# Sixteen experts of a mixture-of-experts stage: the overflow block cut into four short branches, the weight splits taken out of them

## The chip, the cores and the metric

The kernel runs on one core of one Trainium2 chip. The metric is the device time of one launch in microseconds (us), the median of three runs. A profiled execution of the same program gives the trace from which the rows below are taken; its times are read from the start of the profile's span.

## The reference

One layer: differential attention, then a mixture of experts in two levels, both with pre-RMSNorm, modulation and a residual, then a last RMSNorm. The part that the change touches is the mixture of experts over 1024 tokens of 1024 values:

```python
g_idx = jnp.argmax(g_logits, axis=-1)                 # one of 4 groups
top_v, top_i = lax.top_k(e_sel, EXPERT_TOP_K)         # 2 of the 4 experts in that group
hid = jax.nn.silu(jnp.einsum('td,edf->tef', t, w_gate)) * jnp.einsum('td,edf->tef', t, w_up)
hid = hid * gates.astype(hid.dtype)[:, :, None]
y = jnp.einsum('tef,efd->td', hid, w_down)            # 16 experts, d = 1024, f = 512
...
x = x + g2[:, None, :] * y
return rmsnorm(x, norm_final)
```

All inputs are float32. Each token goes to two experts, so 2048 pairs of token and expert are worked on.

## The kernel before

Attention and routing come first (765 us of the span) and are not touched. Then the sixteen experts run one after the other. For expert e the kernel knows the number n of its tokens only at run time, as a register on every engine.

**Slots.** An expert has 128 slots in a main block and 64 more in a small block (M2 = 64); a third block, a loop of 128 slots at a time (over_loop), is there for n > 192. GpSimd gathers the rows of the tokens from h2d by an indirect DMA into xgxa (main) and xgxb (small). A slot without a token points to one of 128 spare rows at the end of h2d and accd, so empty slots are gathered and scattered like full ones. The result of a block, times g2, is added into accd by an indirect DMA with accumulation (scatter_add).

**Pieces.** The weights of an expert come as 12 pieces of 128x1024 float32 (512 KB each): 0 to 3 are gate and up for the first half of f, 4 to 7 for the second half, 8 to 11 are down. Each piece lands in a raw buffer (wraw, 12 of them, NRAW) and is split into a high part whi (a cast on ScalarE, split_hi) and a low part wlo (raw minus high, split_lo), so that TensorE can multiply in three passes of its faster float32r form. The low parts are made by VectorE, but for pieces 8 and 11, which GpSimd makes (PLO). A load into a raw buffer is issued on SyncE's queue once the split that read the buffer is done (split_done, raw_to). The split parts live in 14 slots taken from two pools (slot_tiles).

**One expert on TensorE** (block): 48 matmuls gu of the first half, 48 of the second, with the transposes of the next expert's tokens (xpose) and the matmuls for the slot indices (slots_mm) in between; then the transposes tp of the gated hidden values (hid), and 12 matmuls py of down for each half. What the other engines do meanwhile is placed by hooks: a list of (count, function), where the count is the number of gu matmuls that have been written, so the program's order on every engine is written out by hand. SPL is the table of hooks for the pieces of the next expert, EVAC, SMM, OH, XPH, GAT and CNT are counts of other hooks.

**The branch** (L1531). After the second gu, one conditional (tc.If, n > 128) holds the whole rest of the expert in two arms. The arm that is taken runs the small block woven into the rest of the main block, with two piece splits, the final multiply by g2 on GpSimd and the nested conditional of over_loop (L1475); the Else arm runs the rest of the main block and the same two splits. After both arms two more pieces are split, and the other eight of the next expert are done in its SPL hooks. A hint (mark_branch_hint_location) tells TensorE's sequencer ahead of time where the conditional will go.

**The last expert** (e = 15) runs beside the final RMSNorm: after the last scatter into accd, eight blocks of accd are loaded (norm_load), squared and summed on ScalarE (norm_sum), scaled on VectorE and stored.

## Time and profile before

| what | value |
| --- | --- |
| median of 3 runs | 1263.29 us (1252.71 to 1267.82) |
| the profiled execution, its own time | 1262.4 us |
| the profiled execution, its span | 1260.6 us |
| TensorE busy over the span | 1123.9 us (89%) |
| VectorE busy | 936.9 us (74%) |
| ScalarE busy | 732.4 us (58%) |
| GpSimd busy | 387.0 us (31%) |
| DMA over the span | 205.22 MB, 163 GB/s |

A busy share is an average over the whole span. The experts start at 765.26 us, when the first gu matmul starts, and the last of them starts at 1210.38 us; those two times are the starts of gu matmuls in the timeline of TensorE. The page's chain of waits holds only the last microsecond (a scatter on GpSimd), so the stage has to be read from windows, from the table of waits and from timelines. In a windows row the columns are the length, then for each engine busy us and instructions, then the granted TensorE clock (1.00 is the full level), the mean busy share of the 16 DMA engines, and GB/s. Engines: PE is TensorE, PEld its weight loads, DVE VectorE, ACT ScalarE, POOL GpSimd, SP SyncE; a q behind a name is that engine's sequencer.

### The profile page before, as it was taken

Reading aid. Unit: us, or ns where it says so; the run is one execution under the profiler, and the core shown is the slowest. Engines: PE = TensorE matmul, PEld = TensorE weight load, DVE = VectorE, ACT = ScalarE, POOL = GpSimd, SP = SyncE. Lnnn points to the kernel's source line nnn. Section 1 sums busy time; section 2 is a strip of 40 time slices with the busy share of each in tenths; the row PEclk is TensorE's granted clock in tenths of the full one; section 3 lists DMA queues with packets and bytes.
Section 4 is the critical chain, followed back from the end, with each engine's and each line's share of the span. In section 5 each row is a group of like instructions: output and inputs, shape, how many; then the busy total and the mean of one; then the engine's idle time right before and its main releaser. Section 6 shows DMA issues by size and latency. Waiting matters only on the chain. (4 is left out here: it accounts for less than half of the span.)

```text
span 1260.6 us, 18887 instructions
## 1 busy us (share of the span) xinstructions
PE 1123.9 (89%) x6816; PEld 938.1 (74%) x6816; DVE 936.9 (74%) x1494; ACT 732.4 (58%) x1218; POOL 387.0 (31%) x335
## 2 busy tenths in 40 slices
PE   6989999999999999998999976888888888888982
PEld 6767777777777777776778866787787877788771
DVE  4768788888988677778765567688686867667754
ACT  5465767676676666678553323566464656535544
POOL 3011020111111010116024115545465764435532
PEclk8899999999999999999999987999999988999996
DMA  9612023322323000114238536799697999679737
GB/s 328 197 45 85 22 85 92 94 90 82 92 77 109 30 26 26 42 35 137 76 127 284 187 120 224 239 300 322 209 316 216 335 297 322 194 214 267 203 92 278
DMA packets 153278, 205.22 MB, mean 163 GB/s; under 512 B 11652, under 2 KB 122917, under 8 KB 153138
## 3 DMA queue, kind: packets, MB, share of 16 engines
q1 hardware_dynamic: 146432, 179.86, 44.6%
q0 software_dynamic: 6512, 23.06, 7.8%
q8 instruction: 75, 1.23, 0.4%
q14 instruction: 65, 0.53, 0.1%
q10 hardware_dynamic: 194, 0.54, 0.1%
HBM read 175.77 MB, written 27.67 MB: 161 GB/s over the span
## 5 line engine op out<-in xcount | busy, mean ns | idle before, releaser
L1132 DVE TENSOR_TENSOR wlo<-wraw,whi 128x1024 fp32r<-128x1024 f32 x155 | 218.2, 1456 | 33.3 <-issue 17.7
L1386 PE MATMUL gu<-whi,XT 128*128 128x256 f32 x1216 | 211.8, 287 | 3.9 <-DVEq L1475 3.9
L1127 ACT CAST whi<-wraw 128x1024 fp32r<-128x1024 f32 x192 | 188.3, 1048 | 28.3 <-PE py L1418 23.2
L499 ACT ACTIVATE E<-E,mn 128x1024 f32<-128x1024 f32 x128 | 147.1, 1151 | 84.0 <-DVE mn L496 83.8
L1386 PEld LDWEIGHTS gu<-whi,XT 128*128 128x128 f32 x1216 | 176.7, 195 | 8.0 <-ACTq L1475 6.4
L496 DVE CUSTOM_DVE_ANT_0 E<-S,negd 128x1024 f32<-128x1024 f32 x128 | 152.8, 1220 | 19.4 <-PE S L491 18.8
L1386 PE MATMUL gu<-wlo,XT 128*128 128x256 f32 x704 | 152.2, 294 | 14.0 <-DVE wlo L1132 12.5
L143 POOL TENSOR_TENSOR wl<-wraw,wh 128x1024 fp32r<-128x1024 f32 x21 | 50.4, 2399 | 333.6 <-ACT wh L142 293.2
L297 PE MATMUL mm<-hH,wh 128*128 128x512 f32 x336 | 139.2, 414 | 2.1 <-DVE V L397 2.1
L297 PE MATMUL mm<-hL,wh 128*128 128x512 f32 x336 | 140.3, 417 | 0.0
L297 PE MATMUL mm<-hH,wl 128*128 128x512 f32 x336 | 138.6, 412 | 0.0
L1132 POOL TENSOR_TENSOR wlo<-wraw,whi 128x1024 fp32r<-128x1024 f32 x37 | 98.4, 2662 | 91.2 <-ACT whi L1127 91.1
L1386 PEld LDWEIGHTS gu<-wlo,XT 128*128 128x128 f32 x704 | 111.9, 195 | 18.3 <-DVE wlo L1132 16.4
L526 ACT CAST aH<-tp 128x512 fp32r<-128x512 f32 x128 | 74.0, 578 | 73.8 <-PE tp L524 73.5
L510 DVE SCALAR_TENSOR_TENSOR E<-E,r 128x1024 f32<-128x1024 f32 x64 | 85.8, 1341 | 27.8 <-ACT E L508 26.2
L1418 PE MATMUL py<-whi,hid 128*128 128x512 f32 x256 | 95.2, 432 | 10.1 <-issue 6.3
L527 DVE TENSOR_TENSOR aL<-tp,aH 128x512 fp32r<-128x512 f32 x128 | 88.0, 687 | 17.2 <-ACT aH L526 16.0
L524 PE MATMUL tp<-ident,E 128*128 128x128 f32 x512 | 78.3, 276 | 10.5 <-DVE aL L527 7.2
L524 PEld LDWEIGHTS tp<-ident,E 128*128 128x128 f32 x512 | 62.3, 141 | 33.6 <-DVE aL L527 13.7
L706 PE MATMUL mm<-wo,wh 128*128 128x512 f32 x240 | 79.6, 406 | 1.3 <-ACT mm L718 1.3
L297 PEld LDWEIGHTS mm<-hH,wh 128*128 128x128 f32 x336 | 63.4, 189 | 18.3 <-issue 5.1
L297 PEld LDWEIGHTS mm<-hL,wh 128*128 128x128 f32 x336 | 63.4, 189 | 17.2 <-issue 8.3
(348 smaller groups left out, 2355.4 us busy)
## 6 DMA issues: line engine op xcount, KB each, us to landing
wraw<-in_expert_w_gate SPq DMA_DIRECT2D x64, 512.0 KB
wraw<-in_expert_w_up SPq DMA_DIRECT2D x64, 512.0 KB
wraw<-in_expert_w_down SPq DMA_DIRECT2D x64, 512.0 KB
aw<-in_ada_w SPq DMA_DIRECT2D x64, 256.0 KB
wraw<-in_attn_w_in SPq DMA_DIRECT2D x23, 512.0 KB
ld<-in_ada_w SPq DMA_DIRECT2D x32, 256.0 KB
ld<-in_x SPq DMA_DIRECT2D x8, 512.0 KB
xt<-in_x SPq DMA_DIRECT2D x8, 512.0 KB
```

The lines of the kernel that those rows point to most:

```text
L297: nc.tensor.matmul(pq, w[:, k], t[k][:, n], start=(k == 0 and i == 0), stop=(k == KT - 1 and i == 2))
L496: nc.vector.tensor_tensor_reduce(out=e, in0=sps[m], in1=negd[:, w0:w0 + S], op0=OP.add, op1=OP.min, scale=-slope, scalar=3.0e38, accum_out=mn)
L499: nc.scalar.activation(e, e, AF.Exp, bias=mn, scale=-1.0, accum_out=sm)
L510: nc.vector.scalar_tensor_tensor(es[0], es[1], r2, es[0], op0=OP.mult, op1=OP.add)
L524: nc.tensor.transpose(pt[:, i], a[:, k * P:(k + 1) * P], ident)
L526: nc.scalar.copy(th[:, kk * 4:kk * 4 + 4, q], pt)
L527: nc.vector.tensor_tensor(tl[:, kk * 4:kk * 4 + 4, q], pt, f(th[:, kk * 4:kk * 4 + 4, q]), op=OP.subtract)
L706: nc.tensor.matmul(py, w[:, h], wt[h][:, ns], start=(h == 0 and s == 0), stop=(h == H - 1 and s == 2))
L1127: nc.scalar.copy(WP[e, i][0], RAW[e, i])
L1132: eng.tensor_tensor(low, RAW[e, i], f(high), op=OP.subtract)
L1386: nc.tensor.matmul(pg[:, i], XT[:, xi, k], w[:, k % 4], start=(k == 0 and xi == 0 and wi == 0 and i == 0), stop=(k == KT - 1 and (xi, wi) ...
L1418: nc.tensor.matmul(py[n], hT[:, xi, i], WP[e, 8 + hf * 2 + i][wi][:, n * 512:(n + 1) * 512], start=(hf == 0 and j == 0), stop=(hf == 1 and ...
```

## The change

- The single conditional is replaced, for experts 0 to 14, by five: over_loop's own (L1486, not taken unless n > 192), now ahead of the small block, and four short ones (all on L1548, function small) that hold only instructions of the small block: (a) its transposes, (b) its first gu, (c) its second gu, the first half of its down and the hid of both, (d) the second half of its down, the multiply by g2 and the scatter. (d) is written into the next expert, at count DSM = 12. The rest of the main block and all splits stand outside. The hint goes to over_loop's conditional; the four short ones have none.
- Six pieces of the next expert are split around the short branches (two ahead of b, two behind b, two behind c); the other six in hooks at counts 0 to 90.
- The 14 slots are made once and used as a ring; there are 11 raw buffers in place of 12.
- All low parts are made by VectorE, so are both halves of the main block's multiply by g2 (before: one half by ScalarE and GpSimd), and the small block's.
- Gathers and scatters get bounds_check = 1023, so the spare rows of empty slots are not moved. The extra 1024 slots of the 3072 that 2048 pairs leave empty are the ones concerned.

The core of the diff:

```diff
-    NRAW = 12
+    NRAW = 11
-    SMM = 80
-    OH = 40
-    NARM = 2
+    SMM = 92
+    OH = 66
...
+    RING = []
     def slot_tiles():
-        pool, nb = (mwr, NEARLY) if nslot[0] % NSLOT < NEARLY else (mw, NSLOT - NEARLY)
-        nslot[0] += 1
-        return [pool.tile([P, 1024], F32R, name=n, bufs=nb) for n in ("whi", "wlo")]
+        j = nheld[0] % NSLOT
+        if j == len(RING):
+            pool = mwr if j < NEARLY else mw
+            RING.append([pool.tile([P, 1024], F32R, name="%s%d" % (n, j)) for n in ("whi", "wlo")])
+        return RING[j]
...
-        eng = eng or (nc.gpsimd if i in PLO else nc.vector)
+        eng = eng or nc.vector
...
-    EVAC = 52
-    N0 = 20
-    SPL = [(0, split_hi, 4), (0, split_lo, 4), (0, split_hi, 5), (0, split_lo, 5), (2, split_hi, 6), (3, split_hi, 7),
-           (30, split_lo, 6), (48, split_hi, 8), (48, split_lo, 8), (50, split_lo, 7), (50, split_hi, 10), (50, split_lo, 10),
-           (69, split_hi, 9), (70, split_lo, 9), (72, split_hi, 11), (80, split_lo, 11)]
+    EVAC = 60
+    DSM = 12
+    N0 = 28
+    SPL = [(0, 6), (24, 7), (56, 8), (64, 9), (80, 10), (90, 11)]
...
+            nc.gpsimd.indirect_dma_start(out=xg[:m], out_offset=None, in_=h2d,
+                                         in_offset=bass.IndirectOffsetOnAxis(ap=idx[:m, b:b + 1], axis=0),
+                                         bounds_check=S - 1, oob_is_err=False)
...
+        over_loop(e, XT, n)
+        s1 = gate(pg1, tt[:, 0, 3:4], P)
+        pt = small_pt()
+        small(lambda: small_evac(small_pe(xs, pt), XT))
+        d = down(e, py, 0, h0, P)
+        take(d, 9)
+        h1 = hid(s1, P)
+        run(d)
+        splits(2)
+        sl, hs = mp.tile([P, 256], F32, name="sl"), mp.tile([P, 2, 2, P], F32R, name="hs")
+        pg = gu_tile()
+        small(lambda: gate(run(gu(e, XT, 0, M2, pg=pg)), g, M2, xs[:, 0:512], sl))
+        splits(2)
+        run(down(e, py, 1, h1, P))
...
+        def small_c():
+            hid(sl, M2, hT=hs)
+            gate(run(gu(e, XT, 1, M2, pg=pg2)), g, M2, xs[:, 512:1024], sl)
+            run(down(e, spy, 0, hs, M2))
+            hid(sl, M2, hT=hs)
+
+        def small_d():
+            for n in range(2):
+                run(down(e, spy, 1, hs, M2, (n,)))
+                fold(spy, oyo, n)
+                r = slice(n * 512, (n + 1) * 512)
+                v.tensor_tensor(oyo[:M2, r], oyo[:M2, r], g2b[:M2, r], op=OP.mult)
+            scatter_add(idx[:M2, 1:2], oyo[:M2])
+
+        small(small_c)
+        splits(2)
+        later.append((DSM, lambda: small(small_d)))
...
-            v.tensor_tensor(yo[:, 0:512], py[0], g2b[:, 0:512], op=OP.mult)
...
-                nc.gpsimd.tensor_tensor(yo[:, 512:1024], yo[:, 512:1024], g2b[:, 512:1024], op=OP.mult)
+            for n in range(2):
+                v.tensor_tensor(yo[:, n * 512:(n + 1) * 512], py[n], g2b[:, n * 512:(n + 1) * 512], op=OP.mult)
```

On VectorE, from the gate of the second half (sl) on, this stood in the Else arm and behind the join of the two arms before; wlo is a split's low part, the L1531 row is the end of the conditional:

```order
L1399 SCALAR_TENSOR_TENSOR sl<-sl,tt,gu 128x256
L1409 TENSOR_TENSOR hid<-tp,hid 128x256
L1132 TENSOR_TENSOR wlo<-wraw,whi 128x1024 x2
L1531 UNCONDITIONAL_BRANCH
L1132 TENSOR_TENSOR wlo<-wraw,whi 128x1024 x5
L1242 TENSOR_SCALAR rk<-rk 128x192 x8
```

and this stands there now, from hid on; the L1548 rows are the short conditionals b and the start of c:

```order
L1419 TENSOR_TENSOR hid<-tp,hid 128x256
L1134 TENSOR_TENSOR wlo_7452<-wraw,whi_7451 128x1024
L1134 TENSOR_TENSOR wlo_7466<-wraw,whi_7465 128x1024
L1548 COMPARE_AND_BRANCH
L1406 TENSOR_TENSOR xgxb<-xgxb,gu 64x512
L1409 SCALAR_TENSOR_TENSOR sl<-sl,tt,xgxb 64x256
L1548 UNCONDITIONAL_BRANCH x2
L1134 TENSOR_TENSOR wlo_7480<-wraw,whi_7479 128x1024
L1134 TENSOR_TENSOR wlo_7489<-wraw,whi_7488 128x1024
L1548 COMPARE_AND_BRANCH
```

Passes over weights that stood in one row of five behind the join stand in pairs between the short branches.

On TensorE, at the end of the second gu, an expert had one conditional, whose arm for n > 128 begins with the small block's transposes (xt from xgxb):

```order
L1386 MATMUL gu<-whi,XT 128x256 x2
L1531 COMPARE_AND_BRANCH
L1296 MATMUL xt<-ident,xgxb 128x64 x8
L1418 MATMUL py_8721<-whi,hid 128x512
L1418 MATMUL py_8721<-wlo,hid 128x512
```

Now the join of over_loop's conditional (L1486) and the first short one stand there in a row, and the down matmuls behind them are common to both cases:

```order
L1486 UNCONDITIONAL_BRANCH x2
L1548 COMPARE_AND_BRANCH
L1303 MATMUL xt<-ident,xgxb 128x64 x8
L1548 UNCONDITIONAL_BRANCH x2
L1428 MATMUL py_8634<-whi_7312,hid 128x512
L1428 MATMUL py_8634<-wlo_7313,hid 128x512
```

The second unconditional row of each pair is on the way that skips a body: it comes behind a wait for all of TensorE's earlier matmuls.

On GpSimd, behind the join of an expert, a piece's low part and half of the multiply by g2 (yo) stood between the gather of the small block and the scatter:

```order
L1274 DMA xgxb<-h2d,ix 64x1024
L1132 TENSOR_TENSOR wlo<-wraw,whi 128x1024
L1590 TENSOR_TENSOR yo<-yo,g2b 128x512
L1432 DMA accd<-yo,ix 1152x1024
L1641 TENSOR_LOAD rk
```

Now the two scatters stand there with the fourth short conditional around the first:

```order
L1274 DMA xgxb<-h2d,ix 64x1024
L1548 COMPARE_AND_BRANCH
L1442 DMA accd<-oyo,ix 1152x1024
L1548 UNCONDITIONAL_BRANCH
L1548 ISA
L1548 UNCONDITIONAL_BRANCH
L1442 DMA accd<-yo,ix 1152x1024
L1640 TENSOR_LOAD rk
```

No pass over a 128x1024 or 128x512 tile is left on GpSimd there.

## Rows read from the trace of the kernel before

**Rows 1.** Windows: whole stage, experts 0, 2, 4, 6, 7-10, 9, 11-14, 15.

```profile
765.26:1210.38 445.12, 385.88 (x2758) 348.04 (x2757) 324.12 (x424) 244.59 (x372) 230.66 (x207) 0.95 0.86 257
765.26:794.25 28.99, 23.10 (x150) 21.33 (x149) 18.84 (x23) 13.71 (x21) 15.88 (x23) 0.86 0.62 211
820.91:843.68 22.77, 19.61 (x149) 17.55 (x148) 20.30 (x25) 14.49 (x22) 12.31 (x12) 1.00 1.03 305
868.61:903.55 34.94, 32.18 (x241) 28.97 (x240) 24.41 (x35) 18.39 (x31) 12.49 (x13) 1.00 0.79 245
929.24:962.20 32.96, 31.83 (x242) 28.79 (x240) 22.39 (x35) 17.76 (x31) 16.04 (x14) 1.00 0.82 255
962.20:1062.86 100.66, 83.72 (x592) 75.73 (x593) 78.30 (x101) 59.27 (x86) 63.36 (x55) 0.92 1.02 309
1014.47:1036.52 22.05, 19.84 (x149) 18.11 (x148) 18.04 (x25) 14.50 (x22) 13.33 (x12) 0.98 1.05 313
1062.86:1210.38 147.52, 132.32 (x945) 118.51 (x944) 99.94 (x131) 76.14 (x122) 61.52 (x50) 0.98 0.73 213
1210.38:1260.60 50.22, 22.55 (x124) 18.70 (x124) 27.95 (x28) 23.83 (x39) 19.37 (x16) 0.74 0.62 210
```

**Rows 2.** Waits of TensorE in 765.26 to 1210.38: us in total, times, longest.

```profile
PE tp L1405 <- DVE sl L1399: 17.6, 6, 3.8
PE py L1418 <- POOLq L1531: 12.8, 3, 5.8
PE gu L1386 <- DVE wlo L1132: 9.5, 10, 1.2
PE py L1418 <- issue: 6.3, 2, 3.4
PE gu L1386 <- DVEq L1475: 3.2, 5, 0.8
```

**Rows 3.** Groups by line, same stretch: busy, mean ns, then idle before.

```profile
L1132 DVE TENSOR_TENSOR wlo<-wraw,whi 128x1024 fp32r<-128x1024 f32 x147 | 207.3, 1459 | 31.9 <-issue 17.7 <-ACT whi L1127 13.2 <-DMA wraw<-in_expert_w_down 1.1
L1132 POOL TENSOR_TENSOR wlo<-wraw,whi 128x1024 fp32r<-128x1024 f32 x31 | 83.6, 2699 | 81.0 <-ACT whi L1127 81.0
L1590 POOL TENSOR_TENSOR yo<-yo,g2b 128x512 f32<-128x512 f32 x14 | 27.7, 1978 | 0.5 <-ACT yo L1589 0.3
L1585 DVE TENSOR_TENSOR yo<-py,g2b 128x512 f32<-128x512 f32 x14 | 9.5, 679 | 0.0
```

**Rows 4.** Timelines of VectorE and GpSimd: start, us, what, idle before.

```profile
809.77 0.42 DVE L1409 TENSOR_TENSOR hid<-tp,hid 128x256 fp32r<-128x256 f32 x1 [1.10 <-issue]
810.72 2.38 DVE L1132 TENSOR_TENSOR wlo<-wraw,whi 128x1024 fp32r<-128x1024 f32 x2 [0.53 <-ACT whi L1127]
...
839.30 3.21 DVE L1132 TENSOR_TENSOR wlo<-wraw,whi 128x1024 fp32r<-128x1024 f32 x1 [0.52 <-DMA wraw<-in_expert_w_down]
...
839.06 2.36 POOL L1132 TENSOR_TENSOR wlo<-wraw,whi 128x1024 fp32r<-128x1024 f32 x1
```

**Rows 5.** Timeline of TensorE at the end of expert 4, where over_loop's conditional is skipped.

```profile
902.09 0.39 PE L1418 MATMUL py<-wlo,hid 128*128 128x512 f32 x1
902.32 0.63 PE L1418 MATMUL py<-whi,hid 128*128 128x512 f32 x2
903.55 0.47 PE L1386 MATMUL gu<-whi,XT 128*128 128x256 f32 x2 [0.60 <-DVEq L1475]
```

**Rows 6.** TensorE's branches, ns least/median/most: L1531 (all), L1475 (958 to 963).

```profile
L1531 PEldq COMPARE_BRANCH  x16: 84/403/5503, 785.1 to 1238.4; - x16
...
L1475 PEldq COMPARE_BRANCH  x2: 191/1302/2414, 958.2 to 961.8; - x2
```

**Rows 7.** Timeline of TensorE in expert 4's small block, gu to the second transposes.

```profile
895.60 0.39 PE L1386 MATMUL gu<-wlo,XT 128*128 128x256 f32 x2
895.83 0.39 PE L1418 MATMUL spy<-whi,hs 128*128 128x512 f32 x1
...
898.49 0.33 PE L1405 MATMUL tp<-ident,sl 64*128 64x64 f32 x2
```

**Rows 8.** DMA queues in 794.25 to 1210.38: packets, MB, share of 16 engines.

```profile
q1 hardware_dynamic: 67307, 88.58, 66.6%
q0 software_dynamic: 5328, 18.88, 19.7%
```

**Rows 9.** Loads of accd for the last norm, on SyncE's queue: ns, then first and last start.

```profile
L1363 SPq DMA_DIRECT2D wraw<-accd x8: 329/387/757, 1225.6 to 1229.3; - x8
```

More of the change, by code (lines that the diff above doesn't have):

```diff
@@ L1388, in gu, with gate @@
         return pg
-    def gate(pg, g, R, lo=None):
-        sl = mp.tile([P, 256], F32, name="sl")
+    def gate(pg, g, R, lo=None, sl=None):
+        sl = mp.tile([P, 256], F32, name="sl") if sl is None else sl
         if R == M2:
@@ L1400, in gate, with hid @@
         return sl
-    def hid(sl, R, name="hid", bufs=2):
+    def hid(sl, R, name="hid", bufs=2, hT=None):
         ph = mps.tile([P, 2, P], F32, name="tp")
@@ L1474, in over_loop @@
         tc.no_sync_barrier()
-        with tc.If(n > P + M2):
+        with tc.If(n > P + M2, label="over%d" % e):
             v.memset(bs, float(P + M2))
@@ L1566, in block @@
-        if last:
-            return
-        with arm.Else():
-            s1 = gate(pg1, tt[:, 0, 3:4], P)
-            d = down(e, py, 0, h0, P)
-            take(d, 7)
-            h1 = hid(s1, P)
-            splits()
-            run(d)
-            run(down(e, py, 1, h1, P))
-        split_done(NARM)
-        nx = [divmod(j, NP) for j in range(nsplit[0], nsplit[0] + (2 if e < NE - 2 else 0))]
-        for j in nx:
-            split_hi(*j)
-            split_lo(*j)
-        split_done(len(nx))
+            n = cnts[e]
@@ new lines, in block, with small @@
+            tc.no_sync_barrier()
+            with tc.If(n > P, label="small%d" % e):
+                pt = small_pe(XG[e, 1])
+                small_evac(pt, XT)
+                over_block(e, XT, idx[:, 1:2], tt[:, 1, 3:4], M2, XG[e, 1])
+                over_loop(e, XT, n)
+            return
+        upto(199)
+        n = cnts[e]
+        g = tt[:, 1, 3:4]
+        xs = XG[e, 1]
+        def small(what):
+            tc.no_sync_barrier()
+            with tc.If(n > P):
+                what()
@@ new lines, in block @@
+        splits(2)
+        run(down(e, py, 1, h1, P))
+        pg2 = gu_tile("idx")
+        spy = [mps.tile([P, 512], F32, name="spy%d" % n, tag="xt", bufs=2) for n in range(2)]
+        def small_c():
[10 more added lines that the diff above has]
+            scatter_add(idx[:M2, 1:2], oyo[:M2])
@@ L1622, in first_smm @@
         ns[1] = slots_mm(1, 2, oh1[0])
-        XG[1, 0] = gather(ns[1][0], 0, "xa")
+        XG[1, 0] = gather(ns[1][0], 0)
     if S1 == 2:
@@ L1641, in load_cnt @@
             cnts[e] = nc.values_load(cnt[0:1, e:e + 1], min_val=0, max_val=S)
-            tc.mark_branch_hint_location("small%d" % e, cnts[e] > P, engines=[mybir.EngineType.PE])
+            what, first = ("over", P + M2) if e < NE - 1 else ("small", P)
+            tc.mark_branch_hint_location("%s%d" % (what, e), cnts[e] > first, engines=[mybir.EngineType.PE])
         hooks = [(CNT, load_cnt)] + later
@@ L1673, in gat @@
             def gat(e=e):
-                XG[e + 2, 0] = gather(ns[e + 2][0], 0, "xa")
+                XG[e + 2, 0] = gather(ns[e + 2][0], 0)
             hooks += [(OH, lambda e=e, oh=oh: oh.append(slots(e + 2, 2))), (SMM, smm), (GAT, gat)]
         if 0 < e < NE - 1:
-            for c, what, i in SPL:
-                hooks.append((c, lambda e=e, i=i, what=what: what(e, i)))
-            hooks.append((SPL[-1][0], lambda: split_done(8)))
+            hooks += [(c, lambda: split_to(nsplit[0] + 1)) for c, i in SPL]
         if e == NE - 2:
@@ L1690, in gat1 @@
             def gat1(e=e):
[L1691 removed]
+                XG[e + 1, 1] = gather(ns[e + 1][0], 1)
             later.append((0 if e < NE - 2 else 30, gat1))
```

92 lines of the change are left out of this document (24 added, 68 removed).

## The prediction

> **What bounds the kernel now.** The chain of waits is of no use here: it ends in one scatter of a microsecond. So I read the windows first, an expert at a time, to see how long each takes and how much of it TensorE works; then TensorE's waits, for what holds it in the rest; then VectorE's passes, DMA and the branches. The stage of experts 0 to 14 takes 445.12 us, of which TensorE works 385.88 at a mean clock of 0.95 [rows 1]. Experts 4, 6 and 11 to 14 run the small block (their windows hold the small block's transposes, 48 in all, eight for each). These six take 34.94 + 32.96 + 147.52 = 215.4 us, 35.9 each; expert 0 takes 29.0; the eight others without it 445.1 - 215.4 - 29.0 = 200.7 us, 25.1 each. At full clock TensorE's work is 19.6 us without the small block (expert 2) and 31.8 with it (expert 6) [rows 1]. So 5.5 us of an expert without it, and 4.1 of one with it, are waits and the lower clock that follows long ones.
>
> TensorE's waits have three large causes [rows 2]. 17.6 us go to the gate on VectorE (sl), six times by up to 3.8 us; they stand in the experts behind small blocks, where five passes over weights in a row are ahead of the gate on VectorE (order of before). 12.8 us go to GpSimd, three times, where the second down needs a low part that GpSimd makes late. 9.5 us go to low parts of VectorE. 6.3 us are "issue", where TensorE's sequencer sat in a branch: the conditional L1531 took up to 5.5 us there [rows 6].
>
> VectorE is the second engine that is nearly full: 20.3 of 22.8 us in expert 2, 18.0 of 22.1 in expert 9 [rows 1]. One of its passes over a piece takes 1.19 us alone (2.38 for two), but 3.21 while GpSimd's own pass of 2.36 runs at the same time [rows 4]; so the mean is 1459 ns over 147 passes [rows 3]. The DMA engines are the third: share 1.02 over experts 7 to 10, 0.73 over 11 to 14 [rows 1]; but nobody waited for a weight load for more than 1.1 us in all [rows 3].
>
> **The change part by part.**
>
> *GpSimd's passes to VectorE.* GpSimd loses 31 passes of 2.70 us and 14 multiplies of 1.98 [rows 3], and with them the 12.8 us for which TensorE waited. VectorE gets two passes more per expert, 2 x 1.19, and a multiply of 0.68 [rows 3, 4]: 3.1 us. It gets back what GpSimd cost it: (1.459 - 1.19) x 10 passes = 2.7 us for an expert on the mean. From expert 9 (25 VectorE instructions in 18.04 us, 10 of them passes) its work becomes 18.0 + 3.1 = 21.1 us at most, 18.4 at least; I take 20.0, since expert 9 had less than the mean share of collisions (GpSimd busy 13.3 us, against 63.36 / 4 = 15.8 for experts 7 to 10). The pass is thus nearly free for VectorE, but it takes up the slack that VectorE had.
>
> *Four short branches and the loop's own.* An expert without the small block now skips five bodies where it skipped one arm. The trace shows what a skip of such a body costs TensorE: at the end of expert 4 the last pair of down matmuls starts at 902.32, at 0.235 us apiece the next would start at 902.79, and it starts at 903.55 [rows 5]: 0.76 us, because the way around a body first waits for all earlier matmuls and then branches with an empty queue. Here I pay it in four places (the loop's and the first short one adjoin: 0.76 + 0.6; the others 0.76 each): 3.6 us. That is TensorE alone: 19.6 + 3.6 = 23.2 us. In one with the small block only the loop's body is skipped, as before. The other engines pay little: their skips are a branch and a semaphore, which I put at 0.15 us each, an estimate from 0.60 us on the row of rows 5 in which VectorE's way and TensorE's both ended, so 0.7 us for VectorE over five.
>
> [...]
>
> *An expert without the small block.* VectorE: 20.0 of work, 0.7 of skips, 1.1 in which it waits for TensorE and ScalarE to hand it hid, and about twice 0.5 in which it waits for ScalarE's high part [rows 4]: 22.8 us. TensorE: 23.2. The two hand each other work five times an expert, so neither reaches its sum; with 0.3 on top I take 23.5, against 25.1 now: 8 x 1.6 = 12.8 us less. The lower bound is 22.5, the upper 25.
>
> *An expert with it.* TensorE: 31.8, 0.76 for the loop's skip, and a new gap in branch c: between its second gu and its second transposes lie only eight down matmuls, 8 x 0.235 = 1.9 us, while the gate's chain took 898.49 - 895.99 = 2.5 [rows 7]; before, three more matmuls filled it. So 0.6 more: 33.2. VectorE: 22.4 in expert 6 [rows 1] plus 2 passes and three multiplies of 0.68 = 26.8 at most, and 24.1 without collisions. It was idle for 33.0 - 22.4 = 10.6 us there; the pairs of passes that now stand between the branches fill about 3 of it. 26.8 - 0.8 + 7.6 = 33.6. With half a microsecond to one for the hand-over I take 34.3, against 35.9: 6 x 1.6 = 9.6 us less. That also pays for the 17.6 us of gates, since the five passes in a row are gone; what is late next is again the gate, but by about 1 us, behind the last two SPL hooks (counts 80 and 90).
>
> *Empty slots.* 1024 gathered rows and some 400 scattered ones fall away. GpSimd's queue held DMA for 19.7% of 416.1 us = 82 us in 5328 packets [rows 8], 15 ns for each: 1.3 us of DMA time for an expert. No wait in rows 2 is for a gather, so I cost it at nothing on the path. Its cover is on the other side: weights take 66.6% of 416.1 us for 14 experts = 19.8 us each, rows 5.9 - 1.3 = 4.6, so 24.4 us of DMA for an expert against my 23.5; in runs of four the 11 raw buffers ahead carry the lack of 4 us. One raw buffer less is a twelfth of that lead.
>
> *Ring, hooks, SyncE.* The ring changes who waits for a slot, not when it is read. SyncE passes five branches without a wait of its own in them. GpSimd's gather of the small block now stands behind the way around the loop's body, which waits until the gather before has landed; it is then some 10 us ahead of its reader. I cost these at nothing, with up to 1 us an expert if that lead goes.
>
> *Expert 0 and the end.* Expert 0 has the low clock of 0.86 and the same kinds of waits; with four passes fewer than the others I take 26.5, so 2.5 less. Expert 15 with the end takes 50.2 us [rows 1], but it is set by the last scatter: the loads of accd start at 1225.6 [rows 9], 15.2 us behind the expert's start, and everything after hangs on them. Two scatters must still land one behind the other; the small one is now short. I take 1 us off.
>
> Sum: 12.8 + 9.6 + 2.5 + 1 = 25.9 us. The profiled execution took 1262.4 us, of which 1260.6 are its span, and the median of the runs is 1263.3, so no shift between the two is needed: 1262.4 - 25.9 = 1236.5, say **1236**. With the bounds of the two kinds of experts (22.5 to 25 and 33.3 to 35.5) this case alone reaches from about 1224 to 1250.
>
> **The rivals.**
>
> *Cheap skips.* If the wait for earlier matmuls hides most of a skip (TensorE would wait there anyway for hid or a low part), VectorE alone is the bound: 22.3 us and 33.3, expert 0 in 25: 8 x 2.8 + 6 x 2.6 + 4 + 1 = 43 us less, **1219**. For it: expert 9 ran in 22.05 already. [...] Against it: rows 5.
>
> *The branches take it back.* L1531's conditional stalled by a median of 0.4 and up to 5.5 us, mostly where DMA was full [rows 6]. If five of them cost 5 us in place of my 3.6 and the loop's jump still stalls, experts without the small block stay at 24.8 and those with it come to 35: 8 x 0.3 + 6 x 0.9 + 1 = 9 us less, **1254**.
>
> *DMA becomes the bound.* Then experts without the small block go at 24.4 and the sum is 7 us smaller: **1243**. For it the share of 1.02; against it that loads are never waited for now, and that the six with the small block leave a quarter of the time free.
>
> *Slower: jumps that miss.* At L1475 of expert 6 one jump took 2.41 us [rows 6], hidden then by matmuls queued ahead; now the queue is empty behind each way around. There are 9 x 5 + 6 = 51 skips. If each stalls for 2.4 us and half of them do, 25 x 2.4 = 60 us come on top of 1236: **1296**. It turns to slower by over 2% (1288) from 22 of the 51 on. [...] Against it: the short bodies are 8 to 40 matmuls long, and the jumps of L1531 that stalled went over some 250.
>
> **How the numbers follow.** The forecast has 0.42, cheap skips 0.20, branches that take it back 0.20, DMA 0.10, slower 0.08. Two per cent of 1263 is 25 us (about what a measurement of this kernel can tell from no change): faster is below 1238. That line runs through my forecast: 0.25 of its 0.42 lies below. With most of the first rival (0.19) and a little of DMA (0.03) faster gets 0.47, slower 0.08, within 2% the rest, 0.45. The range leaves out the slower case and the outer half of the fast one: 1214 to 1261. The forecast's own is 1224 to 1250.
>
> **What would show it.** Windows of experts without the small block at 23 to 24 us and of those with it at 34 to 35; no pass over a weight on GpSimd and VectorE's mean pass at 1.2 us; the waits for the gate (17.6) down to under 8 and those for GpSimd at nothing; four gaps of about 0.6 us on TensorE at the short branches; GpSimd's DMA packets down by about a quarter. I am wrong if a skip costs TensorE under 0.4 or over 1.1 us, if a branch stalls often by over 2 us, or if TensorE waits for a gather or a load.

## The result, and the profile after

The changed kernel takes 1269.8 us in the median (1264.7 to 1275.6, 20 runs), the kernel before 1263.3 (1252.6 to 1273.1, 20 runs): ratio 1.0064, with a 95% interval of 1.0043 to 1.0084. It is slower by 0.6%, where 2% faster was forecast, and outside the range. The profiled execution has a span of 1268.6 us.

The windows of the changed kernel, with the columns of [rows 1]: the whole stage, expert 0, 4, 6, experts 8 to 10, 11 to 14, and 15 with the end.

```profile
763.28:1215.89 452.61, 394.78 (x2751) 349.49 (x2749) 324.16 (x477) 238.20 (x356) 116.80 (x157) 0.92 0.79 244
763.28:795.52 32.24, 26.37 (x150) 23.29 (x149) 16.86 (x25) 14.38 (x22) 12.51 (x20) 0.76 0.56 185
866.12:902.48 36.36, 32.05 (x232) 28.79 (x233) 23.69 (x36) 16.30 (x27) 7.37 (x10) 0.91 0.80 248
930.04:967.15 37.11, 32.65 (x233) 29.31 (x233) 25.12 (x37) 17.55 (x28) 7.37 (x10) 0.91 0.82 256
990.95:1057.94 66.99, 60.86 (x445) 53.15 (x445) 58.57 (x85) 42.98 (x61) 22.17 (x30) 1.00 1.04 337
1057.94:1215.89 157.95, 135.76 (x937) 121.68 (x937) 100.34 (x149) 72.78 (x116) 28.72 (x35) 0.89 0.64 194
1215.89:1268.60 52.71, 21.83 (x133) 18.89 (x132) 28.97 (x33) 23.83 (x40) 11.43 (x13) 0.72 0.53 191
```

Read against [rows 1]: the eight experts 1 to 3, 5 and 7 to 10, without a small block, take 452.61 - 32.24 - 231.42 = 188.95 us, 23.6 each, from 25.1. The forecast was 23.5. The six with one take 36.36 + 37.11 + 157.95 = 231.42, 38.6 each, from 35.9; the forecast was 34.3. Expert 0 takes 32.2 (forecast 26.5, before 29.0), and the end 52.7 (before 50.2). So the gain came and was given back in three places, the experts with a small block above all. The clock tells the same: 0.92 over the stage from 0.95, and 394.78 us busy for about as many matmuls as took 385.88.

TensorE's ten largest waits in that stage, to be held against [rows 2]:

```profile
PE xt L1303 <- DMA accd<-yo,ix: 10.6, 2, 6.3
PE xt L1303 <- DVE sl L1409: 7.2, 2, 3.6
PE xt L1303 <- DMA xgxa<-h2d,ix: 6.1, 1, 6.1
PE tp L1415 <- DVEq L1548: 5.7, 6, 1.0
PE py L1428 <- PEq L1548: 4.6, 8, 0.6
PE py L1428 <- ACTq L1548: 4.1, 1, 4.1
PE tp L1415 <- DVE sl L1409: 3.5, 6, 0.6
PE py L1428 <- PEq L1486: 3.0, 1, 3.0
PE py L1428 <- issue: 3.0, 1, 3.0
PE xt L1303 <- ACT sl L1408: 3.0, 1, 3.0
```

The three old causes are gone or small: the gate from 17.6 to 3.5, GpSimd's low parts of down from 12.8 to nothing (GpSimd still makes two low parts of expert 0, and TensorE waits 2.5 us for one of them). In their place stand six waits of the transposes of branch a (xt, L1303), one in each expert with a small block: 10.6 + 7.2 + 6.1 + 3.0 = 26.9 us. Four different releasers are named for one and the same wait, so the names alone do not tell what was waited for. All six stand right behind the conditional of the third block's loop (L1486), which no expert here enters. What the engines do at that line, from its own view (ns least/median/most, then first and last start); the last row is expert 12 alone:

```profile
L1486 PEldq COMPARE_BRANCH  x15: 356/462/4653, 782.0 to 1190.8; - x15
L1486 POOLq COMPARE_BRANCH  x15: 45/53/53, 785.0 to 1193.7; - x15
L1486 POOLq INC_SWDGE_SEM  x15: 273/716/1184, 785.4 to 1194.4; - x15
...
L1486 POOLq INC_SWDGE_SEM  x1: 1023/1023/1023, 1116.2 to 1116.2; - x1
```

On GpSimd the branch itself is 0.05 us; on TensorE it takes up to 4.65. Behind it GpSimd has an instruction of 0.27 to 1.18 us, INC_SWDGE_SEM. I read it as the posting of the semaphores of the loop's transfers that aren't made: it stands at each of the 15 ways around the loop, and at nine of the 36 skips of a short body, where (d), the one of the four with a transfer of GpSimd, is skipped nine times; and in all six experts the transposes of branch a start 0.2 to 0.5 us after it ends. Expert 12 shows who is late (lines of GpSimd, VectorE, ScalarE and TensorE from one timeline, others left out):

```profile
1111.01 0.40 PE L1396 MATMUL gu<-whi,XT 128*128 128x256 f32 x2
1111.02 2.08 POOL L1442 DMA_INDIRECT accd<-yo,ix  x1 [4.80 <-DVE hid L1419]
1112.74 1.21 DVE L1134 TENSOR_TENSOR wlo<-wraw,whi 128x1024 fp32r<-128x1024 f32 x1
1113.34 0.83 POOL L1262 TENSOR_SCALAR tt<-ax,rk 128x2 f32<-128x2 f32 x1
1114.11 0.38 ACT L1408 ACTIVATE sl<-gu 128x256 f32<-128x256 f32 x1 [3.06 <-DVEq L1486]
1116.01 1.10 POOL L1274 DMA_INDIRECT xgxa<-h2d,ix  x1 [0.61 <-POOLq L1486]
1117.53 1.08 PE L1303 MATMUL xt<-ident,xgxb 64*128 64x64 f32 x8 [6.12 <-DMA xgxa<-h2d,ix]
```

TensorE has done its gu at 1111.41. VectorE still has a pass of its queue to do and is past the loop by 1114. GpSimd first gets a scatter away, then makes the slot numbers of expert 14 and the gather that hangs on them, and posts from 1116.2 to 1117.2; at 1117.53 TensorE goes on. Its transposes read the tile xgxb, into which the loop's body gathers too; that they wait for the posting of these gathers of a body that is not run is what e1 tests. GpSimd is late by itself only in experts 12 and 13. In 4, 6 and 11 it posts behind VectorE: in expert 4 VectorE passes the loop at 882.5, GpSimd posts until 883.2, and TensorE goes on at 883.5. In 14 GpSimd's posting and VectorE's pass end within half a microsecond of each other, ahead of the transposes.

VectorE's pass in the same stage:

```profile
L1134 DVE TENSOR_TENSOR wlo<-wraw,whi 128x1024 fp32r<-128x1024 f32 x179 | 213.3, 1220 | 23.3 <-ACT whi L1129 13.5 <-DVEq L1548 5.4 <-PE py L1428 2.7
```

It takes 1220 ns, from 1459 in [rows 3], as forecast. GpSimd's DMA queue, as in [rows 8]:

```profile
q0 software_dynamic: 5696, 15.31, 14.3%
```

There it was 19.7%, over the stage without expert 0.

### The profile page after: what moved, and what is told of

Its sections match the earlier page's. It is cut to its first block, busy times and chain, and to the rows that moved or that the text cites. A ratio compares the mean times of both kernels' runs of the same rounds, so it can differ in the third digit from the quotient of the medians.

```text
span 1268.6 us, 19565 instructions
## 1 busy us (share of the span) xinstructions
PE 1130.0 (89%) x6816; PEld 937.1 (74%) x6816; DVE 938.9 (74%) x1552; ACT 726.1 (57%) x1204; POOL 265.6 (21%) x283
## 5 line engine op out<-in xcount | busy, mean ns | idle before, releaser
L1134 DVE TENSOR_TENSOR wlo<-wraw,whi 128x1024 fp32r<-128x1024 f32 x187 | 222.9, 1220 | 35.1 <-ACT whi L1129 25.3
L1129 ACT CAST whi<-wraw 128x1024 fp32r<-128x1024 f32 x192 | 193.2, 1048 | 8.0 <-ACTq L1548 4.6
L1396 PEld LDWEIGHTS gu<-whi,XT 128*128 128x128 f32 x1216 | 172.7, 192 | 9.9 <-issue 6.2
L496 DVE CUSTOM_DVE_ANT_0 E<-S,negd 128x1024 f32<-128x1024 f32 x128 | 152.8, 1220 | 19.2 <-PE S L491 18.4
L1396 PE MATMUL gu<-wlo,XT 128*128 128x256 f32 x704 | 148.4, 289 | 2.5 <-POOL wlo L1134 2.5
L1428 PE MATMUL py<-whi,hid 128*128 128x512 f32 x256 | 102.3, 463 | 16.5 <-PEq L1548 4.6
L527 DVE TENSOR_TENSOR aL<-tp,aH 128x512 fp32r<-128x512 f32 x128 | 88.0, 687 | 17.4 <-ACT aH L526 16.3
L1428 PEld LDWEIGHTS py<-whi,hid 128*128 128x128 f32 x256 | 56.5, 221 | 35.4 <-issue 11.7
L297 PEld LDWEIGHTS mm<-hL,wh 128*128 128x128 f32 x336 | 63.5, 189 | 17.2 <-issue 8.3
```

Of the source, the lines that this page charges most:

```text
L297: nc.tensor.matmul(pq, w[:, k], t[k][:, n], start=(k == 0 and i == 0), stop=(k == KT - 1 and i == 2))
L496: nc.vector.tensor_tensor_reduce(out=e, in0=sps[m], in1=negd[:, w0:w0 + S], op0=OP.add, op1=OP.min, scale=-slope, scalar=3.0e38, accum_out=mn)
L527: nc.vector.tensor_tensor(tl[:, kk * 4:kk * 4 + 4, q], pt, f(th[:, kk * 4:kk * 4 + 4, q]), op=OP.subtract)
L1129: nc.scalar.copy(WP[e, i][0], RAW[e, i])
L1134: eng.tensor_tensor(low, RAW[e, i], f(high), op=OP.subtract)
L1396: nc.tensor.matmul(pg[:, i], XT[:, xi, k], w[:, k % 4], start=(k == 0 and xi == 0 and wi == 0 and i == 0), stop=(k == KT - 1 and (xi, wi) ...
```

## The experiments

Twelve kernels ran. The stage is experts 0 to 14, the end is expert 15 and what follows; both are read off the profiled execution, from the first gu of expert 0 and of expert 15. Ratios are to the kernel before on the same chip. A profiled execution need not lie at its kernel's median: that of e1 is 3.4 us under it, those of e9 and e12 are 5 us above.

| kernel | median us | ratio (95%) | stage | end |
|---|---|---|---|---|
| before | 1263.3 | 1 | 445.1 | 50.2 |
| changed | 1269.8 | 1.0064 (1.0043 to 1.0084) | 452.6 | 52.7 |
| e1: own buffer | 1259.0 | 0.9955 (0.9928 to 0.9981) | 435.9 | 52.5 |
| e2: no third block | 1222.3 | 0.9656 (0.9626 to 0.9687) | 402.9 | 53.4 |
| e3: late branch of expert 14 in its own expert | 1272.5 | 1.0069 (1.0039 to 1.0098) | 452.9 | 50.7 |
| e4: e1, loop nested in branch a | 1267.5 | 1.0032 (1.0005 to 1.0059) | 450.3 | 52.4 |
| e5: third blocks at the end | 1224.7 | 0.9668 (0.9649 to 0.9688) | 403.5 | 58.5 |
| e6: short loop body | 1252.5 | 0.9886 (0.9867 to 0.9906) | 435.5 | 52.7 |
| e7: e2, GpSimd's passes back | 1231.5 | 0.9720 (0.9699 to 0.9741) | 412.0 | 52.6 |
| e8: e2, no bounds | 1223.9 | 0.9671 (0.9641 to 0.9702) | 403.0 | 54.9 |
| e9: e1 and e6 | 1227.8 | 0.9705 (0.9661 to 0.9750) | 412.3 | 52.7 |
| e10: before, no third block | 1254.7 | 0.9927 (0.9897 to 0.9957) | 436.8 | 51.8 |
| e11: e2, no late branch | 1226.2 | 0.9702 (0.9668 to 0.9736) | 406.6 | 51.1 |
| e12: e5, one pass an expert on GpSimd | 1249.1 | 0.9877 (0.9840 to 0.9914) | 425.1 | 58.7 |

**e1, a buffer of its own for the loop's gather.** The loop's gather goes into the yo buffer, and the gather that filled xgxb again behind the loop goes; no conditional moves.

```diff
-                xl = XG[e, 1]
+                xl = mp.tile([P, D], F32, name="xl", tag="yo")
...
-            if e < NE - 1:
-                gather(ns[e][0], 1)
```

> One edit to the changed kernel: the third block's loop gathers into the yo buffer instead of the small block's buffer, so that branch a's transposes no longer wait for GpSimd to have passed over that loop; every conditional stays where it is. Theory A (GpSimd, late behind the scatter, the slot numbers and the first gather, holds branch a at the loop's skip): the six gaps ahead of branch a (3.55, 3.65, 4.21, 6.12, 6.34, 2.97, together 26.8 us) end where ScalarE's activation starts after VectorE's pass, 0.5 to 3.3 us sooner each and 9.4 us in all, and the slow-clocked matmuls behind the long ones shrink by 2 to 3 us: 1257 to 1261 us. Theory B (the price is that of TensorE's own skips, five an expert): gaps unchanged, 1269 to 1271. Theory C (VectorE is what is late at that skip, with two splits queued ahead of it): what is left of the gaps is 2.4 to 3.1 us in each of the six.

Theory A's time came: 1259.0. TensorE's wait for xt is now one row, and the event that holds TensorE ahead of the transposes shrinks. The waits row and the line's own view are of this kernel:

```profile
PE xt L1303 <- DVEq L1486: 16.1, 6, 2.8
```

```profile
L1303 PEldq EVENT_SEMAPHORE  x7: 51/1816/2331, 883.0 to 1183.7; - x7
```

In the changed kernel that second row read:

```profile
L1303 PEldq EVENT_SEMAPHORE  x27: 51/51/5553, 883.1 to 1195.9; - x27
```

27 semaphore events became 7, and the longest wait 2.3 us instead of 5.6. The wait for GpSimd is shown: the waits ahead of branch a fall from 26.9 to 16.1 us, and in all six experts the transposes now start before GpSimd's posting has ended. What is left is much the same in all six experts, 2.4 to 2.8 us, and its releaser is VectorE passing L1486: theory C holds beside A. VectorE's queue is long there, and branch a's PSUM tile (xt) is also read by VectorE in the loop's body; e9, without these transposes, shows that the wait belongs to the body, and that it is this tile is read from the code.

**e2, no third block.** `over_loop(e, XT, n)` is left out for experts 0 to 14.

> The changed kernel without the third block's loop in experts 0 to 14 (that block is left out of the computation; no expert of these inputs needs it): one conditional less an expert, four short branches stay. Theory A with C (engines are late at this conditional): branch a waits for its own gather and for VectorE's evacuation of XT alone, so the six gaps fall from 26.8 us to about 1.5 each, ScalarE's 3.0 us wait for VectorE at the second gate goes in all 15 experts, the skip's 0.57 us on TensorE goes nine times, and expert 0's 3.05 us gap: 1236 to 1246 us. Theory B (all skips cost alike): one of five skips goes, 15 times 0.6 to 0.8, that is 9 to 12 us: 1258 to 1261. If the scatters' bounds or the longer VectorE queue were the loss, it stays near 1265.

It gave more than any theory had: 1222.3 us, with a ratio 0.041 under that of the changed kernel. Its windows (stage, expert 0, 4, 6, 11 to 14), then TensorE's wait for xt, and its branches at the short conditionals:

```profile
764.08:1166.93 402.85, 378.51 (x2750) 337.02 (x2749) 322.96 (x477) 238.37 (x356) 115.58 (x157) 0.98 0.87 273
764.08:790.68 26.60, 23.12 (x150) 20.91 (x149) 16.35 (x25) 13.79 (x21) 12.54 (x20) 0.86 0.66 217
855.79:888.00 32.21, 30.47 (x233) 27.61 (x233) 24.91 (x37) 17.58 (x28) 7.39 (x10) 1.00 0.92 295
910.98:943.37 32.39, 30.46 (x232) 27.76 (x232) 24.99 (x37) 17.56 (x28) 7.39 (x10) 1.00 0.98 318
1032.06:1166.93 134.87, 128.84 (x936) 116.13 (x937) 99.75 (x149) 72.76 (x116) 28.87 (x35) 0.97 0.74 228
```

```profile
PE xt L1303 <- PE gu L1396: 5.1, 6, 0.9
```

```profile
L1548 PEldq COMPARE_BRANCH  x84: 70/179/438, 782.7 to 1167.8; - x84
```

The gaps ahead of branch a are 0.9 us each; no branch of TensorE takes over 0.44 us; expert 0 takes 26.6, those with a small block (32.21 + 32.39 + 134.87) / 6 = 33.2, the other eight (402.85 - 26.60 - 199.47) / 8 = 22.1. TensorE is busy for 378.51 us instead of 394.78 with the same work, at a clock of 0.98 instead of 0.92: of the 49.8 us of the stage, 16.3 are this, given back where the long waits went.

**e3, expert 14's last branch at home.**

```diff
-        later.append((DSM, lambda: small(small_d)))
+        if e < NE - 2:
+            later.append((DSM, lambda: small(small_d)))
+        else:
+            small(small_d)
```

> The changed kernel with one edit: expert 14's last small branch (its second half down, folds and scatter) stands in its own expert, as before the change, and not behind twelve matmuls of expert 15; the other experts keep it late. Theory D (the end grew by 2.5 us since the last scatter into the accumulator left 14 us after expert 15's start instead of 8.5, and the row loads wait for it): expert 14 gets 1 to 2.5 us longer for the wait on the second half's transposes, the stretch from expert 15's first gate matmul to the end shrinks by 3 to 5 us: 1266 to 1269. If the end is set by something else, the end does not move and the time is 1270 to 1272.

The end shrank by 2.0 us, less than the 3 to 5 expected, and expert 14 grew by 0.6. The time did not fall; the intervals of the two overlap. The window of the end:

```profile
1220.76:1271.50 50.74, 20.41 (x125) 17.65 (x123) 27.42 (x31) 21.17 (x37) 12.34 (x13) 0.72 0.55 198
```

So the late scatter does lengthen the end (50.74 is the 50.22 of before, [rows 1]), but it is 2 us of what went wrong, and the run can't tell a net gain.

**e4, the loop nested in branch a.**

```diff
-        over_loop(e, XT, n)
-        s1 = gate(pg1, tt[:, 0, 3:4], P)
-        pt = small_pt()
-        small(lambda: small_evac(small_pe(xs, pt), XT))
+        s1 = gate(pg1, tt[:, 0, 3:4], P, sl=oyo[:, 0:256])
+
+        def small_a():
+            over_loop(e, XT, n)
+            small_evac(small_pe(xs), XT)
+
+        small(small_a)
```

> The own-buffer edit of the run before, and the third block's conditional nested in branch a, with the second gate ahead of it (into the first 256 columns of the small block's output tile). Experts without a small block then skip four branches instead of five. Theory A with B's price of a skip: the own buffer's 9 to 12 us, and nine experts lose one skip of 0.57 us, 5 us: 1252 to 1257. If all engines' late pass of the loop's skip is only moved to branch a's skip, the nine experts keep their length (22.2 to 23.8) and the time is that of the own buffer alone.

This was a miss: 1267.5, above e1. TensorE's branches at the short conditionals of this kernel (L1545 here, L1548 in the changed one):

```profile
L1545 PEldq COMPARE_BRANCH  x84: 70/180/6468, 783.9 to 1216.5; - x84
```

One conditional fewer is passed, but the jump over branch a now goes over the loop's body as well, and single jumps take up to 6.5 us, where those at the short conditionals took up to 1.7 in e1 and 0.44 in e2. That pointed to the length of what is jumped over, which e6 tests. The run also moves the second gate ahead of the branch, so it shows no price by itself.

**e6, a short body.** The one line of the loop's body that runs its block is left out, so the third block isn't computed. With the line the body's transposes went too, which the expectation still counted: what is left of the body is VectorE's one-hots, eight slot matmuls, the slot numbers and the gather into xgxb.

```diff
-                over_block(e, run(xpose(xl, XT)), ix[:, 0:1], tx[:, 0, 3:4], P)
```

> The changed kernel with the third block's gate, down and scatter left out of its loop: the conditional stays, with the slot numbers, the gather into the small block's buffer and eight transposes as its body, so some 250 fewer TensorE instructions to jump over. Theory A (waiting for late engines at the skip): TensorE's branch at the skip falls under 1 us everywhere (1.9 to 4.65 us in five experts of the changed kernel) and the gaps of experts 0, 3 and 5 (3.05, 3.02, 4.14) fall under 1, but the gaps ahead of branch a stay within 1 us of what they were, since GpSimd's gather is still in the body: 1254 to 1261. Theory J (it is the jump over a long body that costs): the gaps ahead of branch a fall under 1.5 us too: 1232 to 1245.

Theory A, and both its halves; the time, 1252.5, is a little under its range. The branch of TensorE at the loop, and its waits:

```profile
L1486 PEldq COMPARE_BRANCH  x15: 231/242/373, 782.1 to 1177.2; - x15
```

```profile
PE xt L1303 <- DMA xgxa<-h2d,ix: 19.5, 4, 6.1
PE xt L1303 <- DMA accd<-yo,ix: 3.9, 1, 3.9
PE xt L1303 <- DMA accd<-oyo,ix: 2.0, 1, 2.0
```

The jump falls from at most 4.65 us to at most 0.37, and the stage from 452.6 to 435.5, while the six waits ahead of branch a still make 25.4 us. The long jumps and the wait for GpSimd are two prices. One jump stayed long, at a short conditional of expert 2: 2.75 us.

**e9, both edits.**

> Both edits in one: the third block's loop gathers into a buffer of its own, and its gate, down and scatter are left out of its body. If the wait for GpSimd (own buffer alone: 10.9 us under the changed kernel) and TensorE's long jumps (short body alone: 17.3 us) are two separate prices, they add up: 1238 to 1246, and what is left over the run without the third block (1222.3) is VectorE's late pass, with gaps ahead of branch a of 2.7 us against 0.92, and one skip more in each expert. If both edits cure the same wait, 1250 to 1254.

They gave more than their sum: the stage is 40.3 us shorter, where e1 alone had 16.7 and e6 17.2. The row says why:

```profile
PE xt L1303 <- DVE XT L1294: 5.1, 6, 0.9
```

The gaps are 0.9 us and not the 2.7 that were expected. Without transposes in the body VectorE reads no xt there, and with a buffer of its own GpSimd writes no xgxb; so branch a waits for nothing at the loop, and its transposes start before VectorE and GpSimd have passed it. The wait for VectorE (1.8 us more in each of six experts) goes by e6's edit, but that can show only once the longer wait for GpSimd is gone too. The conditional with nothing behind it that anyone waits for costs 412.3 - 402.9 = 9.4 us of stage in the profiled executions, 0.6 an expert; by the medians it is 5.5. A few stalls at short branches are among it (the longest jump 3.2 us, the longest gap 2.0).

**e10, the kernel before without third blocks.**

> The kernel before the change, with the third blocks of experts 0 to 14 left out of the computation. If the third block's place is all that differs in worth between the two forms (the four short branches in themselves gain nothing), it comes to the changed kernel without it: 1220 to 1228. If the short branches, the ring and the passes on VectorE gain what the prediction's steps said (1.6 us in each of 14 experts, 2.5 in expert 0, 1 at the end), it stays 20 to 30 us behind that: 1242 to 1255, with TensorE's seven long jumps (1.9 to 5.5 us in the kernel before) shorter or not by what is left to jump over.

1254.7: the third block cost the form before 0.7%, and the changed form 4.1. So the rest of the change is worth 0.9927 - 0.9656 = 2.7%, some 34 us, once the loop is out of the way. Its waits are still those of [rows 2]:

```profile
PE tp L1405 <- DVE sl L1399: 18.1, 8, 3.7
PE gu L1386 <- DVE wlo L1132: 14.5, 17, 1.2
```

**e7, e8, e11: parts of the change, on e2.** GpSimd makes the low parts of pieces 8 and 11; the bounds go from the gathers and scatters; the late branch stands in its own expert.

```diff
-        eng = eng or nc.vector
+        eng = eng or (nc.gpsimd if i in (8, 11) else nc.vector)
```

> The run without the third block (left out here too), with the subtractions of pieces 8 and 11 on GpSimd again, as before the change. The prediction's step: with GpSimd's passes beside it a VectorE pass takes 1.46 us in the mean and not 1.22, GpSimd's own 2.7 us; VectorE is relieved of 2.4 us an expert and gets about 10 times 0.24 back. If GpSimd's passes also hold the slot numbers and gathers behind them, and the pieces come late for the second half's down: 1230 to 1242. If VectorE's work is hidden at 22 us an expert, the time stays at 1220 to 1226.

> The run without the third block (left out here too), with the empty slots' rows moved again (gathers and scatters without a bound, as before the change). The prediction's step: empty slots cost nothing on the path: 1220 to 1225, with the first queue's bytes up from 17.7 to 23.1 MB. Rival: a scatter that moves up to 64 more rows lands later, and GpSimd, which waits for a scatter's landing ahead of the next, is late for the slot numbers and gathers: 1226 to 1234.

> The changed kernel without the third block (left out here too), with the last small branch (second half down, folds, scatter) in its own expert in all 15 experts, not behind twelve matmuls of the next. The prediction's step that the late branch saves TensorE the wait for the second half's evacuation: six experts get 1 to 2 us longer, the end 2 us shorter: 1225 to 1232. If that wait is as long in the next expert, or the scatter's earlier landing gives as much back: 1218 to 1223.

All three times lie in the first range of their expectation. GpSimd's passes cost 0.64% (8 us): VectorE's pass goes up to 1376 ns.

```profile
L1134 DVE TENSOR_TENSOR wlo<-wraw,whi 128x1024 fp32r<-128x1024 f32 x149 | 200.1, 1376 | 22.9 <-ACT whi L1129 12.1 <-DVEq L1548 5.6 <-PE py L1428 2.8
```

By the first gu of each expert, experts 8 to 10 became shorter (20.7 us each instead of 21.9) and those behind a small block longer (expert 5 from 23.0 to 27.4, 12 from 33.3 to 40.4): the loss is a net of both. What holds the longer ones was not taken apart. Bounds: no difference that can be told, with 20.19 MB on GpSimd's queue instead of 15.31. Late branch: 0.46% in its favour (6 us), intervals that overlap; stage 3.7 us shorter with it, end 2.3 longer. At home, the branch makes an expert with a small block longer (4 from 32.2 to 34.5 us) and the one behind it shorter (5 from 23.0 to 21.4).

**e5, a whole kernel with the third blocks at the end.** Behind expert 15 stands one conditional on the largest count; in it experts 0 to 14 each have their own, load and split their weights anew, run the loop and finish its rows. Its body is not run with these inputs, so what it takes when it is, is not known.

```diff
-        over_loop(e, XT, n)
...
+    most = nc.values_load(RT0["rk"][0:1, 1253:1254].bitcast(I32), min_val=0, max_val=S)
+    tc.no_sync_barrier()
+    with tc.If(most > P + M2):
+        nc.gpsimd.indirect_dma_start(out=accd, out_offset=bass.IndirectOffsetOnAxis(ap=ns[NE - 1][0][:, 0:1], axis=0),
+                                     in_=XC[0], in_offset=None, bounds_check=S - 1, oob_is_err=False)
+        for e in range(NE - 1):
+            third(e)
```

> A whole kernel again: the changed kernel with the third blocks of experts 0 to 14 behind expert 15, under one conditional on the largest count, where they load and split their weights anew and finish their rows; the inner branches are as in the run without the third block (1222.3 us). If what the third block cost was its conditional amid each expert, and not its presence in the program, the experts keep that run's lengths (small ones 32 to 35 us, others 21.5 to 23.1, expert 0 26.6) and the one skip lies behind the last matmul beside the last rows' way out: 1221 to 1227. If a skip costs by the length of what it jumps over (the body here is fifteen times as long), it shows at the end alone, as 5 us or more between the last matmul and the end over that run's: 1228 to 1235.

1224.7 us: faster than both kernels, by 3.3% than the one before (0.9668, 0.9649 to 0.9688). The stage is that of e2 to 0.6 us, and the time lies in the expectation's first range. Yet the skip does show at the end, as its second range had it:

```profile
1166.01:1224.50 58.49, 22.48 (x133) 19.23 (x132) 28.97 (x33) 23.73 (x40) 12.34 (x13) 0.71 0.49 173
```

```profile
L1732 PEldq COMPARE_BRANCH  x1: 4840/4840/4840, 1202.1 to 1202.1; - x1
...
L1732 POOLq INC_SWDGE_SEM  x1: 1271/1271/1271, 1217.4 to 1217.4; - x1
```

The profiled end is 5.1 us longer than that of e2 (53.4), with GpSimd's posting from 1217.4 on; the medians differ by 2.4 us, within their intervals. TensorE's 4.84 us cost nothing, since it has no work left.

**e12, one pass an expert on GpSimd.** Piece 4 in e5.

> The whole kernel with the third blocks at the end (1224.7 us), with one subtraction an expert on GpSimd: piece 4, split at an expert's end, where GpSimd has nothing else and which TensorE needs 48 matmuls into the next expert. With both passes of the kernel before on GpSimd, experts without a small block took 20.6 us (21.7 without) and those behind a small one lost 4 to 7, where VectorE's one-hot passes and the scatter met GpSimd's passes. If one pass in a quiet place keeps half of that gain and none of the loss: 1217 to 1222. If any GpSimd pass holds VectorE as long as it runs: 1224 to 1232.

A miss, and slower than both ranges: 1249.1. Expert 13 of this kernel, and then of e5:

```profile
1120.85:1158.24 37.39, 35.73 (x241) 31.41 (x240) 25.61 (x39) 18.50 (x30) 11.39 (x12) 0.91 0.72 208
```

```profile
1099.93:1133.54 33.61, 32.13 (x241) 29.07 (x241) 25.41 (x40) 18.51 (x30) 8.56 (x11) 1.00 0.76 230
```

VectorE and ScalarE are as busy as before; what differs is TensorE's granted clock, 0.91 against 1.00, and with it 3.6 us of busy time for the same 241 matmuls. No gap of TensorE in that expert is over 1 us. The stage as a whole is 21.6 us longer, 0.5 to 1.6 us in each expert without a small block. The run shows that the lower clock came with the one pass of under 3 us; why was not found.

## Why the prediction was wrong

- **An expert without a small block**: 23.5 forecast, 23.6 measured. That is right in sum by luck, and not in its parts. The step priced five skips at 3.6 us of TensorE. Experts 8 to 10, at 22.3 us each, have these waits over 0.15 us and no others:

```profile
PE tp L1415 <- DVEq L1548: 2.8, 3, 1.0
PE py L1428 <- PEq L1548: 1.8, 3, 0.6
```

The second row is the place where the loop's conditional and the first short one adjoin: 0.6 us for both, 0.72 from start to start as [rows 5] was read (0.76), where 1.36 was put down. The other short branches leave no gap over 0.15 us; the first row is the gate, late on VectorE. So the skips were mis-sized, and 22.3 is what the rival of cheap skips had (e2, without the loop: 22.1). The mean is raised to 23.6 mostly by stalls that the forecast did not have: in expert 5 the jump at the loop took 4.65 us (a gap of 4.1), and expert 3 stood for 3.0 us behind a short branch ("issue"), with an instruction load in that time; both are gone in e2 and e6.
- **An expert with it**: 34.3 forecast, 38.6 measured. **Here the prediction failed**, in two sentences. "In one with the small block only the loop's body is skipped, as before", with 0.76 for it: before, that skip stood behind the small block at an expert's end ([rows 5]); now it stands ahead of branch a, between two steps of TensorE, in all experts. And, of GpSimd's gather behind the way around the loop's body, "I cost these at nothing, with up to 1 us an expert": the step followed what GpSimd waits for, and not who waits for GpSimd. Branch a does, since the loop's body writes the same tile: it waits 2.97 to 6.34 us in each of the six, 26.9 in all. e1 shows it by the buffer, which takes 10.8 of them away, e6 by the wait that stays when the jump is short; of the 16.1 left, all but 5.1 go when the transposes and what follows them are out of the body too (e9). Without the loop these experts take 33.2, a little under the forecast.
- **What was late next**: the gate by about 1 us, said the step. The gate's waits are 3.5 us in all, 0.6 in each small block, which is the new gap in branch c as forecast. But VectorE with the last two splits behind it was the next to be late, at the loop's skip: 2.7 us (e1).
- **Expert 0**: 26.5 forecast, 32.2 measured, 26.6 without the loop. Its jump at L1486 took 3.7 us; in e6, where it is short, the expert takes 27.3.
- **The end**: 1 us off was forecast, 2.5 on came. Moved behind twelve matmuls of expert 15, the small block's scatter leaves 14 us after the expert's start where the last one left at 8.5. The prediction took the small scatter to be short and did not look at when it starts. e3 gives back 2.0 of it.
- **The rivals**: "jumps that miss" had the stalls, on the wrong bodies: the jump of 2.41 us that it started from has a packet of the instruction queue q8 starting in its time, and so have the four longest over the loop (3.0 to 4.7 us). It let half of 51 skips stall, 36 of which go over short bodies; the branches at the short conditionals take 0.18 us in the median and 1.75 at most, while five of the fifteen jumps over the loop take 1.9 to 4.7 us. The reason it gave against itself, that the stalled jumps of L1531 went over some 250 matmuls, holds for the loop's body, which was in every expert's way now.
- **Right as forecast**: VectorE's pass (1.22 us for 1.2) and GpSimd's passes (e7), empty slots (e8), DMA not the bound (share 1.04 in experts 8 to 10, at 22.3 us each). The queue's bytes fell by a quarter, from 20.19 MB; its packets, which the forecast had a quarter down, not at all (5696 with and without the bounds).
- **The range**: the bounds of the two kinds of experts (22.5 to 25 and 33.3 to 35.5) add up to 1222.5 to 1255.7, where the prediction wrote 1224 to 1250. The measured time is outside of both.

The sum: 11.8 us less in eight experts, 16.0 more in six, 3.2 more in expert 0, 2.5 more at the end, and 2.0 less ahead of the stage: 8.0, and the spans differ by 1268.6 - 1260.6 = 8.0.

What stays open: of the 34 us that the rest of the change is worth without the loop, e7 and e11 account for some 14. How the other 20 divide between the four branches, the ring and the new places of the hooks was not taken apart. The hint, which is at the loop's conditional and at none of the four, was varied in no run.

## What to carry to other kernels

In this kernel a conditional that was never entered still ordered the engines: TensorE, next to touch a tile that the body names, waited until the engines that use that tile in the body had passed around it, GpSimd with its posting as e1 shows (the waits ahead of branch a fall from 26.9 us to 16.1) and VectorE as e9 shows (from 16.1 to 5.1). So ask of every skipped body which tiles it names, who uses them next, and what the engines have queued ahead of the skip; and put a rare, long body where nothing comes after it (here behind the last expert), which made this change worth 3.3%. When a wait has a different releaser in each place, look for what those places have in common in the program.

## What the runs showed of the hardware

- What a branch of TensorE takes does not follow from the length of the jump alone: 231 to 373 ns over a body of eight matmuls (e6), 356 to 4653, with a median of 462, over the whole loop, and 4840 over fifteen of them (e5), hardly more than the longest over one. At the short conditionals it was at most 438 in e2 and e5, but up to 2747 in e6 and 3164 in e9, where the loop's conditional still stands ahead of them. What the long ones share is a load of instructions: in all the traces here, from 760 us on, 28 branches of TensorE took 2.4 us or more, and each has a packet of the instruction queue q8 starting in its time; 35 took 0.6 to 2.2 us, and none of them has. The queue moves more where the long body stands in the experts (first row) than with a short one (second, e6) or none (third, e2), each over its own stage. That a long jump waits for this load is my reading of the two counts; which instructions a jump finds loaded, the traces don't show.

```profile
q8 instruction: 47, 0.77, 0.7%
```

```profile
q8 instruction: 32, 0.52, 0.5%
```

```profile
q8 instruction: 29, 0.48, 0.5%
```

- GpSimd's INC_SWDGE_SEM, read above as the posting for transfers not made, takes 0.27 to 1.18 us at this loop, 1.27 at the end's conditional.
- TensorE's granted clock goes with a third of the difference between the changed kernel and e2: 16.3 of the 49.8 us are busy time for the same matmuls, at a mean of 0.92 instead of 0.98. In expert 12 TensorE stood still from 1111.4 to 1117.5, and from 1113.1 to 1123.2 its granted clock was 0.50.
